# Strassen's seven products for an FFN up projection, and the FFN split into an up phase and a down phase

## The chip, the cores and the metric

One core of a Trainium2 chip runs one inference step of a decoder layer. The metric is the device time of one execution in microseconds, the median of several runs. Matrix products run on TensorE (PE in the profile, its weight loads are PEld), elementwise work on VectorE (DVE), ScalarE (ACT) and GpSimd (POOL); SyncE (SP) issues most DMAs. Matmuls write to PSUM, which the kernel uses in tiles of one or two banks of 512 columns; all else stands in SBUF or in DRAM.

## The reference, cut to what matters

1024 prompt tokens and 8 sample tokens (one each of 8 requests) go through one layer of width 1024. A token mixer (gated delta rule and a convolution branch, merged by gates and projected by `w_out`) is followed by the FFN, in which `T` is 1024 and `D_FF` 2816:

```
x = x + merged @ w_out                         # output projection, residual
h = rmsnorm(x, norm_ffn_w)
u = causal_dwconv(h @ w_up, state, ffn_conv_w) + ffn_conv_b      # width 3 along the tokens, 2*2816 channels
x = x + (silu(u[:, :2816]) * u[:, 2816:]) @ w_down
y = rmsnorm(x, norm_final_w)
```

The last rows of `h @ w_up` are returned as the new convolution state as well. All values are float32.

## The kernel before, in words

Activations lie with channels on the partitions and the 1032 tokens (1024 prompt, 8 sample) along the columns, in three tiles `t` of 344 (`TH`). Every large product is done in three terms: each operand is split into a high part, rounded to the type float32r, and a low part, and `gemm` (L172, its matmul at L182) adds high x high, low weight x high and high weight x low for each 128 rows k of the contraction. A weight tile (8 k of 128x128, 512 KB) comes in two DMAs and is split by `split_w` (L135): ScalarE makes the high part (L140), VectorE the low part (L141).

Matmuls are issued in the order in which the program writes them. A background job (a generator such as `norm2`) writes its own matmuls between those of a gemm: `tick()` (L152) is called after every fourth matmul, and a job that yields n goes on 2n ticks later. The other engines and the DMA queues are ordered by a planner, which takes what it reckons ready, in written order where several are; an engine then works its list strictly in that order, and an instruction that waits holds up those behind it. Tiles of a closed pool give their memory to the pools opened after it; a new tile waits until the readers of the old tiles under it are through.

The output projection (L1171 to L1181) runs t by t over 8 output tiles m; x1 (the residual stream) stays in SBUF. After each t `norm2(t)` (L1155) is spawned: column sums by TensorE, a reciprocal root on VectorE, a broadcast by TensorE, then the scaling and the split into h2hi and h2lo.

The FFN goes through its 22 channel tiles f. `up_pair(f)` (L1245) multiplies two weight tiles, the gate's and the value's, with all three token tiles, each gemm into one PSUM bank out of six (`mmtile2`); ScalarE copies each bank into rg or rv and makes the third tap on the way (L1209, L1210). `up_taps` (L1217) adds the other two taps on VectorE, the sample tokens get theirs from the state, ScalarE applies silu (L1257), VectorE multiplies and splits into yh and yl. After every second tile, `down_mt` (L1301, matmul L1308) adds the previous two tiles' share of the down projection onto x1, for 8 m and 3 t; the last four tiles come at the end, t by t, and `final` (L1328) normalizes each t and stores it.

Of the kernel before, what the change touches and what calls it, by code (L numbers as in the profile page):

```python
# [16 lines left out]
P = 128  # L17
# [17 lines left out]
EPS = 1e-6  # L35
MAGIC = 1597463007.0
# [15 lines left out]
    wod=(KT, P, KT, P), woc=(KT, P, CI, P), wout=(KT, P, KT, P), wup=(2 * NF, P, KT, P), wdn=(NF, P, KT, P),  # L52
# [10 lines left out]
def body(tc, I, O):  # L63
# [20 lines left out]
    with top:  # L84
# [3 lines left out]
        wp = top.enter_context(tc.tile_pool(name="wp", bufs=2, side="left", **R))  # L88
        ap = top.enter_context(tc.tile_pool(name="act", bufs=1, side="left", **R))
        mmp = top.enter_context(tc.tile_pool(name="mmp", bufs=2, space=PSUM, **R))  # L90
# [147 lines left out]
        d_vn = dram.tile([NH, NB, P], F32, name="d_vn")  # L238

# [819 lines left out]
        mhi = [ap.tile([P, KT, TH], F32R, tag=f"ahi{t}", name=f"mhi{t}") for t in range(NTH)]  # L1059
        mlo = [ap.tile([P, KT, TH], F32R, tag=f"alo{t}", name=f"mlo{t}") for t in range(NTH)]  # L1060
# [21 lines left out]
        for m in range(KT):  # L1082
# [13 lines left out]
            if m == KT - 2:  # L1096
                finish(cj)
                cst.close()
                load_c0()
        sas = (("raw", 2), ("zs", 1), ("raw", 2), ("xs", 1))  # L1100
        for m in range(KT):
            w = next_w()
            for t, (t0, n, npr) in enumerate(th):
                sg = sgp.tile([P, TH], F32, tag="sg", name="sgb")
                nc.sync.dma_start(sg, d_gb[m, :, t0:t0 + TH])
                g, bufs = sas[(NTH * m + t) % 4]
                sa = hp.tile([P, TH], F32, tag=g, name="sa", bufs=bufs)
                nc.sync.dma_start(sa, d_ga[m, :, t0:t0 + TH])
                ps = mmtile()
                gemm(ps, w, ((lambda k: chi[t][k]), (lambda k: clo[t][k])), CI)  # L1110
                stt(sg, sg, 1.0, ps, ALU.add, ALU.mult)
                add(sg, sg, sa)
                nc.scalar.activation(mhi[t][:, m, :], sg, AF.Copy, scale=0.5)
                stt(mlo[t][:, m, :], sg, 0.5, mhi[t][:, m, :].bitcast(F32), ALU.mult, ALU.subtract)
# [5 lines left out]
        fst = ExitStack()  # L1120
        rp_ = fst.enter_context(tc.tile_pool(name="res", bufs=1, side="right", **R))
        x1 = [rp_.tile([P, KT, TH], F32, name=f"x1_{t}") for t in range(NTH)]
        nsp = fst.enter_context(tc.tile_pool(name="nsp", bufs=1, side="right", **R))
        mm2 = fst.enter_context(tc.tile_pool(name="mm2", bufs=4, space=PSUM, **R))
        psn2 = fst.enter_context(tc.tile_pool(name="psn2", bufs=1, space=PSUM, **R))
        alt = dict(i=0)

        def psc_():
            return psn2.tile([P, 3], F32, tag="nrm_c", name="nrm_c")

        def psb_():
            return psn2.tile([P, TH], F32, tag="nrm_b", name="nrm_b")


        def mmtile2():
            alt["i"] += 1
            return (mmp if alt["i"] % 3 == 0 else mm2).tile([P, TH], F32, tag="mm", name="mm")

        nacc = [None] * NTH

        def sq_acc(t, src, m, key):
            if m == 0:
                nacc[t] = nsp.tile([P, TH], F32, tag="nacc", name="nacc", bufs=2)
                nc.scalar.activation(nacc[t], src, AF.Square)
            else:
                sq = nsp.tile([P, TH], F32, tag="nsq", name="nsq", bufs=2)
# [3 lines left out]
        ost = ExitStack()  # L1150
        op_ = ost.enter_context(tc.tile_pool(name="op", bufs=2, side="right", **R))
        wo = [None] * KT
        h2hi, h2lo = [None] * NTH, [None] * NTH

        def norm2(t):  # L1155
            yield 3
            rb = yield from col_rsqrt_g(nsp, psc_, psb_, nacc[t], TH, 1.0 / D)
            h2hi[t] = ap.tile([P, KT, TH], F32R, tag=f"ahi{t}", name=f"h2hi{t}")
            h2lo[t] = ap.tile([P, KT, TH], F32R, tag=f"alo{t}", name=f"h2lo{t}")
            for k in range(KT):  # L1160
                hh = nsp.tile([P, TH], F32, tag="hh", name="hh", bufs=2)
                stt(hh, x1[t][:, k, :], nrm[:, 1, k:k + 1], rb, ALU.mult, ALU.mult)
                split(h2hi[t][:, k, :], h2lo[t][:, k, :], hh)

        n2j = None

        def load_wo(m):
            wo[m] = load_w(I["wout"][m], wp) if m < 2 else load_w(I["wout"][m], op_, f"oh{m}", f"ol{m}", 1)

        load_wo(0)  # L1170
        for t, (t0, n, npr) in enumerate(th):  # L1171
            for m in range(KT):
                if t == 0 and m + 1 < KT:
                    load_wo(m + 1)
                xs = op_.tile([P, TH], F32, tag="xs", name="xs")
                nc.sync.dma_start(xs, I["xT"][m, :, t0:t0 + n])
                ps = mmtile2()
                gemm(ps, wo[m], ((lambda k: mhi[t][:, k, :]), (lambda k: mlo[t][:, k, :])), KT)
                add(x1[t][:, m, :], ps, xs)
                sq_acc(t, x1[t][:, m, :], m, "n2")  # L1180
            n2j = spawn(norm2(t))  # L1181
        ost.close()

# [9 lines left out]
        G = 2  # L1193
        ups = [I["wup"][i] for i in range(2 * NF)]
        yh, yl, wd = {}, {}, {}
        upw = {}

        def get_up(i):
            if i < 2 * NF and i not in upw:
                upw[i] = load_w(ups[i], wp)  # L1200

        def h2rhs(t):
            return (lambda k: h2hi[t][:, k, :]), (lambda k: h2lo[t][:, k, :])

        def up_mm(i, raw, acc):
            nc.gpsimd.memset(raw[:, 0:FW - 1], 0.0)

            def ev(t, ps, t0, n, npr):
                nc.scalar.copy(raw[:, FW - 1 + t0:FW - 1 + t0 + npr], ps[:, 0:npr])  # L1209
                nc.scalar.activation(acc[:, t0:t0 + npr], ps[:, 0:npr], AF.Identity, bias=cfb[:, i:i + 1],  # L1210
                                     scale=cfw[:, i, 2:3])
                if t == 2:
                    nc.scalar.copy(stf[:, i, :, FW - 1], ps[:, npr:n])  # L1213

            return ev

        def up_taps(i, raw, acc, lo=0, hi=T):  # L1217
            for j in (1, 0):
                stt(acc[:, lo:hi], raw[:, lo + j:hi + j], cfw[:, i, j:j + 1], acc[:, lo:hi], ALU.mult, ALU.add)
            if hi < T:  # L1220
                return
            nc.gpsimd.tensor_copy(fpo[:, i, :], raw[:, T:T + FW - 1])
            pr = fp_.tile([P, NB, FW], F32, tag="fpr", name="fpr", bufs=2)
            mul(pr, stf[:, i], cfw[:, i, :].unsqueeze(1).to_broadcast([P, NB, FW]))
            nc.vector.tensor_reduce(out=acc[:, T:NT], in_=pr, op=ALU.add, axis=mybir.AxisListType.X)
# [226 lines left out]
```

## Time and profile before

| | us |
|---|---|
| median of 3 runs (lowest, highest) | 1866.91 (1866.83, 1866.99) |
| span of the profiled execution | 1863.8 |
| TensorE busy in it | 1836.3 |
| VectorE, ScalarE, GpSimd busy | 1245.1, 824.1, 101.4 |

The profiled execution is one of its own; its span is the time from its first to its last instruction, and the device time of a run has a few microseconds around it. A busy matmul record covers the time to its modelled end, so neighbouring records overlap; the time that one adds to a stream is the distance from its start to the next start.

### The profile page before, as it was taken

Reading aid. Unit: us, or ns where it says so; the run is one execution under the profiler, and the core shown is the slowest. Engines: PE = TensorE matmul, PEld = TensorE weight load, DVE = VectorE, ACT = ScalarE, POOL = GpSimd, SP = SyncE. Lnnn points to the kernel's source line nnn. Section 1 sums busy time; section 2 is a strip of 40 time slices with the busy share of each in tenths; the row PEclk is TensorE's granted clock in tenths of the full one; section 3 lists DMA queues with packets and bytes.
Section 4 is the critical chain, followed back from the end, with each engine's and each line's share of the span. In section 5 each row is a group of like instructions: output and inputs, shape, how many; then the busy total and the mean of one; then the engine's idle time right before and its main releaser. Section 6 shows DMA issues by size and latency. Waiting matters only on the chain.

```text
span 1863.8 us, 33240 instructions
## 1 busy us (share of the span) xinstructions
PE 1836.3 (99%) x12607; PEld 1816.9 (97%) x12607; DVE 1245.1 (67%) x3222; ACT 824.1 (44%) x2090; POOL 101.4 (5%) x245
## 2 busy tenths in 40 slices
PE   7999999999999999999999999999999999999997
PEld 7899999999999999999999999999999999999997
DVE  7998798689868986745447556445545545555567
ACT  5565456555655565544223235242243243234241
POOL 4300020001000100000000000000000000000000
PEclk9999999999999999999999999999999999999999
DMA  4233213222322243335556212011011011012012
GB/s 163 64 124 103 88 69 118 89 75 86 123 91 75 88 128 96 114 121 176 165 180 204 93 62 74 18 68 52 18 68 58 23 57 69 22 47 68 34 48 92
DMA packets 114112, 163.66 MB, mean 88 GB/s; under 512 B 31968, under 2 KB 68768, under 8 KB 113952
## 3 DMA queue, kind: packets, MB, share of 16 engines
q1 hardware_dynamic: 106896, 153.07, 25.3%
q10 hardware_dynamic: 7056, 8.47, 1.3%
q8 instruction: 99, 1.62, 0.4%
q14 instruction: 61, 0.50, 0.1%
HBM read 128.20 MB, written 33.29 MB: 87 GB/s over the span
## 4 chain that ended last, share of the span: by engine, by line
PE 93%; DVE 4%; ACT 1%; DMA 1%; issue 0%; SPq 0%; DVEq 0%; ACTq 0%
PE mm L182 71%; PE mm L1308 13%; PE tr L659 1%; PE tr L746 1%; PE psS L824 1%; DVE cacc L78 1%; PE po L831 1%; PE tr L724 1%; PE pv L815 1%; PE po L821 1%; PE pk L810 1%; DVE xt L78 1%; PE tr L787 0%; PE tr L797 0%; PE tr L901 0%
## 5 line engine op out<-in xcount | busy, mean ns | idle before, releaser
L182 PE MATMUL mm<-hhi,whi 128*128 128x344 f32 x1360 | 449.8, 331 | 11.4 <-ACT whi L81 6.9
L182 PE MATMUL mm<-hhi,wlo 128*128 128x344 f32 x1360 | 449.7, 331 | 2.5 <-DVE wlo L75 2.4
L182 PE MATMUL mm<-hlo,whi 128*128 128x344 f32 x1360 | 440.3, 329 | 0.0
L182 PE MATMUL mm<-h2hi,whi 128*128 128x344 f32 x1056 | 337.2, 319 | 0.0
L182 PE MATMUL mm<-h2hi,wlo 128*128 128x344 f32 x1056 | 336.6, 319 | 0.0
L182 PE MATMUL mm<-h2lo,whi 128*128 128x344 f32 x1056 | 336.3, 319 | 0.0
L140 ACT CAST whi<-wraw 128x512 fp32r<-128x512 f32 x276 | 164.6, 626 | 308.3 <-PE mm L1308 188.3
L182 PEld LDWEIGHTS mm<-hhi,whi 128*128 128x128 f32 x1360 | 258.9, 190 | 15.3 <-ACT whi L81 7.4
L182 PEld LDWEIGHTS mm<-hhi,wlo 128*128 128x128 f32 x1360 | 259.0, 190 | 4.8 <-DVE wlo L75 3.7
L182 PEld LDWEIGHTS mm<-hlo,whi 128*128 128x128 f32 x1360 | 257.2, 190 | 0.5
L141 DVE TENSOR_TENSOR wlo<-wraw,whi 128x512 fp32r<-128x512 f32 x272 | 184.7, 688 | 96.7 <-ACT whi L140 94.8
L72 DVE TENSOR_TENSOR x<-x,mm 128x344 f32<-128x344 f32 x240 | 120.4, 511 | 137.8 <-PE mm L1308 137.8
L182 PEld LDWEIGHTS mm<-h2lo,whi 128*128 128x128 f32 x1056 | 198.2, 188 | 0.0
L182 PEld LDWEIGHTS mm<-h2hi,whi 128*128 128x128 f32 x1056 | 198.2, 188 | 0.0
L182 PEld LDWEIGHTS mm<-h2hi,wlo 128*128 128x128 f32 x1056 | 198.2, 188 | 0.0
L78 DVE SCALAR_TENSOR_TENSOR cacc<-u,ccw,cacc 128x512 f32<-128x512 f32 x240 | 172.9, 743 | 0.6 <-ACT cacc L563 0.5
L1308 PE MATMUL mm<-yh,whi 128*128 128x344 f32 x480 | 153.3, 319 | 0.0
L1308 PE MATMUL mm<-yl,whi 128*128 128x344 f32 x480 | 153.3, 319 | 0.0
L1308 PE MATMUL mm<-yh,wlo 128*128 128x344 f32 x480 | 153.0, 319 | 0.0
L182 PE MATMUL mm<-og,whi 128*128 128x344 f32 x512 | 123.2, 321 | 0.0
L78 DVE SCALAR_TENSOR_TENSOR ag<-rg,cfw,ag 128x1024 f32<-128x1024 f32 (+2 forms) x48 | 57.3, 1195 | 49.4 <-ACT stf L1213 48.3
L1308 PEld LDWEIGHTS mm<-yh,whi 128*128 128x128 f32 x480 | 90.3, 188 | 0.0
(325 smaller groups left out, 3046.5 us busy)
## 6 DMA issues: line engine op xcount, KB each, us to landing
wraw<-in_wup SPq DMA_DIRECT2D x88, 256.0 KB, 2.6
wraw<-in_wdn SPq DMA_DIRECT2D x44, 256.0 KB, 2.7
gr<-d_gc SPq DMA_DIRECT2D x16, 512.0 KB, 3.7
xt<-in_xT SPq DMA_DIRECT2D x12, 344.0 KB, 6.4
d_ga<-sg ACTq DMA_DIRECT2D x24, 172.0 KB, 2.1
d_gb<-sg ACTq DMA_DIRECT2D x24, 172.0 KB, 1.9
sga<-d_ga SPq DMA_DIRECT2D x24, 172.0 KB, 2.3
d_ga<-sga SPq DMA_DIRECT2D x24, 172.0 KB, 3.8
```

What stands on the lines that cost most here:

```text
L72: nc.vector.tensor_tensor(out=out, in0=a, in1=b, op=ALU.add)
L78: nc.vector.scalar_tensor_tensor(out=out, in0=a, scalar=s, in1=b, op0=op0, op1=op1)
L140: nc.scalar.copy(hi[:, k:k + 4], raw)
L141: weng["e"].tensor_tensor(out=lo[:, k:k + 4], in0=raw, in1=hi[:, k:k + 4].bitcast(F32), op=ALU.subtract)
L182: nc.tensor.matmul(ps, lhs[:, k, :], r(k), start=k == 0 and i == 0, stop=k == kt - 1 and i == 2)
L659: nc.tensor.matmul(gv[:, i, :], kT[:, cs[c]], kT[:, cs[c]], start=True, stop=True)
L724: nc.tensor.matmul(gv[:, i, :], kT[:, cs[c]], qT[:, cs[c]], start=True, stop=True)
L746: nc.tensor.transpose(gv[:, i, :], src[:, cs[half * 4 + i]], ident)
L810: nc.tensor.matmul(pk, kT[:, cs[c]], S, start=True, stop=True)
L815: nc.tensor.matmul(pv, tt[:, c, :], vs[:, c, :], start=True, stop=True)
L821: nc.tensor.matmul(po, qT[:, cs[c]], S, start=True, stop=False)
L1308: nc.tensor.matmul(ps, w, y[f][:, t0:t0 + TH], start=n == 0, stop=n == last)
```

## The change: what it does

Let the up weights of a channel tile be cut in four: the gate's and the value's 128 columns, each in an upper and a lower half of the contraction (4 k each): a21 and a22 of the gate, a11 and a12 of the value. The tokens are cut into two halves b of 516 and each of these into two quarters of 258 (`Q`), so that the normalized input has four blocks for each b. Strassen's scheme in its form by Winograd gets the four output blocks (gate and value, by two quarters) from seven block products in place of eight: sums s1 to s4 of weight pieces, differences t1 to t4 of input blocks (b11, t2, b21, t3, t1, t4, n22 in the order of use), and sums of the products. `prod` issues one product for the halves b in its list, 12 matmuls of 258 columns each; products go to three PSUM tiles x, y, z of two banks (one bank for each b), some of them added onto what stands there after that has been read: the order is x, y, x, y, z, y, z, and after the products p1s, u2, c11, u3, c22, c21 and c12 are formed in turn (`EV`). c11 and c12 are value blocks (tile rv), c21 and c22 gate blocks (tile rg).

The output projection works with the same quarters, m by m for each half b: 258 columns instead of 344, its weights loaded once for each b, and it also writes the residual stream to DRAM (`d_x1`). `norm2(b)` then scales X[b] in place and `combos(b)` forms the seven operands, each with a high and a low part; those of b=1 are formed while the first pass runs. That pass is begun with b=0 alone. The activated y of each channel tile goes to DRAM (`d_y`); the sample tokens' taps are formed once at the end for all tiles. After the last tile the up phase's memory is given up, and the down phase runs t by t with the whole contraction in two units of 11 channel tiles (33 matmuls of 344 columns each), h=1 of a tile two steps behind h=0. y is read back from DRAM and split there, the down weights (in a new layout, by output tile) are read and split again for each t, and the residual comes from `d_x1`.

The mixer before it changes only in where mhi and mlo (the output projection's input) stand and how they are cut. The core of the diff:

```diff
+Q = NT // 4
+HB2 = 2 * Q
+KH = KT // 2
+FH = NF // 2
...
+        def norm2(b):
             yield 3
+            p1, p2 = norm_ps()
+            rb = yield from col_rsqrt_g(nsp, p1, p2, nacc[b], HB2, 1.0 / D)
             for k in range(KT):
+                stt(X[b][:, k, :], X[b][:, k, :], nrm[:, 1, k:k + 1], rb, ALU.mult, ALU.mult)
+            if tpool[b] is not None:
+                yield 2
+                yield from combos(b)
...
+        def get_wq(f, j):
...
+            nm = ORD[j][0]
+            if nm[0] == "s":
+                if nm == "s2":
+                    get_sum(f, "s1")
+                src = get_sum(f, nm)
+            else:
+                src = raws[f, nm]
+            h = up_.tile([P, KH, P], F32R, tag="uhi", name="uhi", bufs=7)
+            l = up_.tile([P, KH, P], F32R, tag="ulo", name="ulo", bufs=7)
+            split(h, l, src)
+            wq[f, j] = (h, l)
+
+        def prod(f, j, z, bs, start, stop):
+            wh, wl = wq[f, j]
+            nm = ORD[j][1]
+            for b in bs:
+                n = 0
+                for k in range(KH):
+                    for w, r in ((wh, That), (wl, That), (wh, Tlot)):
+                        nc.tensor.matmul(z[:, b, 0:Q], w[:, k, :], r[b][nm][:, k, :], start=start and n == 0,
+                                         stop=n == 3 * KH - 1, skip_group_check=True)
+                        n += 1
+                        if n % 4 == 0:
+                            tick()
...
+        EV = (e_p1, e_u2, e_c11, e_u3, e_c22, e_c21, e_c12)
+        DST = ("x", "y", "x", "y", "z", "y", "z")
...
+        u = begin(0)
+        for j in range(6):
+            stage(u, j, (0,), j not in (2, 4, 5))
+        finish(n2j[1])
+        nst.close()
...
+        fp_ = fst.enter_context(tc.tile_pool(name="ffn", bufs=1, side="right", **R))
...
+        outs(u)
+        s0 = slice(0, 1)
+        e_c11(u, s0)
+        e_c22(u, s0)
+        e_c21(u, s0)
+        stage(u, 6, (0,))
+        for j in range(7):
+            stage(u, j, (1,))
+            get_wq(1, j)
+        get_raw(2)
+        activate(u)
+        for f in range(1, NF):
+            u = begin(f)
+            outs(u)
+            for j in range(7):
+                stage(u, j, (0, 1))
+                get_wq(f + 1, j)
+            get_raw(f + 2)
+            activate(u)
...
+        for i in range(len(seq)):
...
+            t, m, h = seq[i]
...
+            for f in range(FH):
+                for w, y in ((wh, yh), (wh, yl), (wl, yh)):
+                    nc.tensor.matmul(ps, w[:, f, :], y[:, f, :], start=h == 0 and n == 0,
+                                     stop=h == 1 and n == 3 * FH - 1)
```

## Rows read from the trace of the kernel before

**Rows 1.** The page: busy time of the engines, and TensorE's clock in 40 slices.
```profile
PE 1836.3 (99%) x12607; PEld 1816.9 (97%) x12607; DVE 1245.1 (67%) x3222; ACT 824.1 (44%) x2090; POOL 101.4 (5%) x245
...
PEclk9999999999999999999999999999999999999999
```

**Rows 2.** The page: the chain of waits, share of the span by engine.
```profile
PE 93%; DVE 4%; ACT 1%; DMA 1%; issue 0%; SPq 0%; DVEq 0%; ACTq 0%
```

**Rows 3.** Windows (us, then engines busy, clock, DMA share, GB/s): output projection, FFN, within.
```profile
1010.00:1101.00 91.00, 91.00 (x590) 91.00 (x590) 52.10 (x125) 29.87 (x58) 0.00 (x0) 1.00 0.33 104
1101.00:1850.20 749.20, 749.20 (x4789) 748.66 (x4788) 410.57 (x736) 261.30 (x514) 12.89 (x87) 1.00 0.14 49
1200.00:1800.00 600.00, 600.00 (x3831) 600.00 (x3830) 319.58 (x539) 204.41 (x398) 9.97 (x69) 1.00 0.14 48
```

**Rows 4.** Groups by line: output projection, one of three kinds; busy us, mean ns.
```profile
L182 PE MATMUL mm<-mhi,whi 128*128 128x344 f32 x192 | 61.5, 320 | 0.0
```

**Rows 5.** Timeline of TensorE at the kernel's start, at half clock: start, length.
```profile
17.16 0.49 PE L182 MATMUL mm<-hhi,wlo 128*128 128x344 f32 x1
17.45 0.49 PE L182 MATMUL mm<-hhi,whi 128*128 128x344 f32 x1
```

**Rows 6.** Timeline of weight loads after two matmuls of 2 columns.
```profile
767.06 0.19 PEld L182 LDWEIGHTS mm<-hhi,whi 128*128 128x128 f32 x1
767.17 0.19 PEld L182 LDWEIGHTS mm<-hhi,wlo 128*128 128x128 f32 x1
```

**Rows 7.** Timeline of weight loads: between them runs an ordinary-float matmul of 258 columns.
```profile
765.26 0.19 PEld L182 LDWEIGHTS mm<-hhi,wlo 128*128 128x128 f32 x1
765.48 0.19 PEld L182 LDWEIGHTS mm<-hlo,whi 128*128 128x128 f32 x1
```

**Rows 8.** DMA issues: KB each, median us to landing.
```profile
wraw<-in_wup SPq DMA_DIRECT2D x88, 256.0 KB, 2.6
```

**Rows 9.** Groups of ScalarE instructions by form: busy us, mean ns.
```profile
L140 ACT CAST whi<-wraw 128x512 fp32r<-128x512 f32 x276 | 164.6, 626 | 308.3 <-PE mm L1308 188.3 <-PE mm L182 59.0 <-DMA wraw<-in_wdn 25.8
L1209 ACT COPY rv<-mm 128x344 f32<-128x344 f32 x35 | 15.6, 445 | 39.4 <-PE mm L182 39.3
L1257 ACT ACTIVATE ag<-ag 128x1032 f32<-128x1032 f32 x21 | 22.4, 1068 | 12.9 <-DVE ag L1226 12.9
L563 ACT ACTIVATE cacc<-u,ccv,ccw 128x1024 f32<-128x1024 f32 x4 | 5.0, 1242 | 0.1
```

**Rows 10.** Groups of VectorE instructions by form: busy us, mean ns.
```profile
L72 DVE TENSOR_TENSOR x<-x,mm 128x344 f32<-128x344 f32 x240 | 120.4, 511 | 137.8 <-PE mm L1308 137.8
L141 DVE TENSOR_TENSOR wlo<-wraw,whi 128x512 fp32r<-128x512 f32 x272 | 184.7, 688 | 96.7 <-ACT whi L140 94.8
L78 DVE SCALAR_TENSOR_TENSOR hh<-x,nrm,nrm_b 128x344 f32<-128x344 f32 x16 | 8.6, 566 | 1.1 <-PE nrm_b L219 0.9
L78 DVE SCALAR_TENSOR_TENSOR av<-rv,cfw,av 128x1024 f32<-128x1024 f32 x42 | 53.8, 1280 | 40.2 <-ACT stf L1213 40.2
L69 DVE TENSOR_TENSOR av<-av,ag 128x1032 f32<-128x1032 f32 x21 | 25.8, 1230 | 0.4
```

**Rows 11.** Timeline of VectorE: two low halves in a row.
```profile
1301.92 1.29 DVE L141 TENSOR_TENSOR wlo<-wraw,whi 128x512 fp32r<-128x512 f32 x2 [1.70 <-ACT whi L140]
```

**Rows 12.** Timeline of TensorE after an idle, and the window behind it (clock, DMA, GB/s last).
```profile
57.95 0.42 PE L182 MATMUL mm<-hhi,whi 128*128 128x344 f32 x1 [1.46 <-ACT bas L1003]
...
59.30:62.60 3.30, 3.30 (x15) 3.24 (x14) 3.11 (x9) 0.52 (x2) 2.03 (x2) 0.50 0.45 149
```

**Rows 13.** Timeline of ScalarE in an up pass: waits in brackets.
```profile
1311.98 1.05 ACT L81 CAST yh<-av 128x1032 fp32r<-128x1032 f32 x1 [2.18 <-DVE av L69]
1312.94 0.63 ACT L1210 ACTIVATE ag<-mm,cfb,cfw 128x344 f32<-128x344 f32 x1
```

**Rows 14.** The page: DMA busy tenths and rate in 40 slices.
```profile
DMA  4233213222322243335556212011011011012012
GB/s 163 64 124 103 88 69 118 89 75 86 123 91 75 88 128 96 114 121 176 165 180 204 93 62 74 18 68 52 18 68 58 23 57 69 22 47 68 34 48 92
```

More of the change, by code (lines that the diff above doesn't have):

```diff
@@ L1056, in body @@
             tick()
-        mhi = [ap.tile([P, KT, TH], F32R, tag=f"ahi{t}", name=f"mhi{t}") for t in range(NTH)]
-        mlo = [ap.tile([P, KT, TH], F32R, tag=f"alo{t}", name=f"mlo{t}") for t in range(NTH)]
+        mhi, mlo = [None] * 2, [None] * 2
         c0st = ExitStack()
@@ L1098, in body @@
                 cst.close()
+                ast.close()
+                mp = wst.enter_context(tc.tile_pool(name="mrg", bufs=1, side="left", **R))
+                for b in (1, 0):
+                    mhi[b] = mp.tile([P, KT, HB2], F32R, name=f"mhi{b}")
+                    mlo[b] = mp.tile([P, KT, HB2], F32R, name=f"mlo{b}")
                 load_c0()
@@ L1117, in body @@
         hs.close()
[L1120 to L1129, printed above, removed]
@@ L1170, in body @@
         load_wo(0)
-        for t, (t0, n, npr) in enumerate(th):
+        load_wo(1)
+        n2j = [None, None]
+        for b in range(2):
+            X[b] = xpool[b].tile([P, KT, HB2], F32, name=f"x{b}")
             for m in range(KT):
[L1173 to L1181, printed above, removed]
@@ L1182, in body @@
-        ost.close()
+                load_wo(KT * b + m + 2)
+                xs = nsp.tile([P, HB2], F32, tag="xs", name="xs", bufs=2)
+                nc.sync.dma_start(xs, I["xT"][m, :, b * HB2:(b + 1) * HB2])
+                ps = pw.tile([P, 2, 512], F32, tag="mm", name="mm")
+                for j in range(2):
+                    sl = slice(j * Q, j * Q + Q)
+                    gemm(ps[:, j, 0:Q], wo[KT * b + m],
+                         ((lambda k: mhi[b][:, k, sl]), (lambda k: mlo[b][:, k, sl])), KT)
@@ new lines, in body, with get_raw @@
+        up_ = ust.enter_context(tc.tile_pool(name="upw", bufs=1, side="left", **R))
+        n2j[1] = spawn(norm2(1))
+        raws, sums = {}, {}
+        wq = {}
+        def get_raw(f):
+            if f >= NF:
+                return
+            for nm, i, h in (("a11", 1, 0), ("a21", 0, 0), ("a22", 0, 1), ("a12", 1, 1)):
+                r = up_.tile([P, KH, P], F32, tag="raw", name="raw", bufs=5)
+                nc.sync.dma_start(r, I["wup"][2 * f + i][:, KH * h:KH * h + KH, :])
+                raws[f, nm] = r
@@ new lines, in body, with small, ptile @@
+        get_raw(0)
+        for j in range(7):
+            get_wq(0, j)
+        get_raw(1)
+        pt_ = tmpp
+        def small(f):
+            return [pt_.tile([P, 2, Q], F32, tag=g, name=g, bufs=1) for g in ("p1s", "u2", "u3")]
+        alt = dict(i=0, pool=None)
+        def ptile():
+            alt["i"] += 1
+            if alt["pool"] is not None and alt["i"] % 4 == 0:
+                return alt["pool"].tile([P, 2, 512], F32, tag="mm", name="mm")
+            return pw.tile([P, 2, 512], F32, tag="mm", name="mm")
@@ new lines, in body, with views, begin, outs @@
+        fp_ = None
+        def views(raw):
+            return raw[:, FW - 1:FW - 1 + NT].rearrange("p (b h c) -> p b h c", b=2, h=2)
+        class Tile_:
+            pass
+        def begin(f):
+            u = Tile_()
+            u.f, u.x, u.y, u.z = f, ptile(), ptile(), ptile()
+            u.p1s, u.u2, u.u3 = small(f)
+            return u
+        def outs(u):
+            u.rg = fp_.tile([P, FW - 1 + NT], F32, tag="rg", name="rg")
+            u.rv = fp_.tile([P, FW - 1 + NT], F32, tag="rv", name="rv")
+            u.ag = fp_.tile([P, T], F32, tag="ag", name="ag")
+            u.av = fp_.tile([P, T], F32, tag="av", name="av", bufs=2)
+            nc.gpsimd.memset(u.rg[:, 0:FW - 1], 0.0)
+            nc.gpsimd.memset(u.rv[:, 0:FW - 1], 0.0)
+            u.vg, u.vv = views(u.rg), views(u.rv)
@@ L1346, in body @@
         finish(fj)
-        fst.close()
+        dst_.close()
 def _const():
```

386 lines of the change are left out of this document (228 added, 158 removed).

## The prediction

> **What bounds the kernel now.** I read the page's busy shares and clock first [rows 1]: TensorE is busy 99% of the span and its granted clock stands at 0.9 or more in every slice. The chain of waits says the same, 93% of it is TensorE [rows 2]. The windows then give the part that is changed [rows 3]: from 1101.00 to 1850.20 us (the FFN) and in the output projection before it TensorE is busy for the whole stretch, while VectorE is busy 410.6 of 749.2 us and ScalarE 261.3. So nothing but TensorE's stream counts there today; each matmul removed is worth its start-to-start time, and each new wait of TensorE costs its full length. The price of one: the FFN's 749.20 us hold 4789 matmuls, 156.4 ns each, and the 600.00 us within it 3831, 156.6; a few are norm matmuls [rows 3]. I use 0.1563 us. The recorded 320 ns of one [rows 4] is longer because matmuls overlap.
>
> **The stream of matmuls.** Before, an up pass (one of 22) has 2 weights x 3 token tiles x 8 k x 3 split terms = 144 matmuls of 344 columns, 3168 in all: 495.2 us. The down projection has 8 x 3 x 22 x 3 = 1584: 247.6 us. The output projection has 576, 192 of each kind [rows 4]: 90.0 us. After, a pass has 7 products x 2 token halves x 4 k x 3 terms = 168 matmuls of 258 columns, 3696 in all; down stays at 1584 of 344; the output projection becomes 2 x 8 x 2 x 24 = 768 of 258. Columns fall by an eighth in the up projection and by nothing elsewhere; the count rises. So all hangs on what a 258-column matmul of this type costs, and no row of before has one. Bounds: scaled by columns from 344 it is 156.3 x 258/344 = 117.2 ns. If instead the 12.9 ns above 344 columns at 2.4 GHz (143.3 ns) is a fixed part, it is 107.5 + 12.9 = 120.4 ns. At 1.2 GHz the same form runs 287 ns apart, exactly its columns with nothing on top [rows 5], which speaks for neither: whatever costs the 12.9 ns shows at the high clock alone. Below, the weight loads set a floor: after two matmuls of 2 columns the next two loads start 0.11 us apart [rows 6]. An ordinary-float matmul of 258 columns has 0.22 us from load to load [rows 7]: twice 258 columns at 2.4 GHz is 215 ns, so it looks like two streamings of 110 ns or less, almost without a fixed part. Above, if the load of 128 weight columns and the moving columns share one supply, 472 columns in 156.3 ns make 386 columns 127.8 ns. I take the middle of the two extrapolations of the same form, 118.8 ns; ends 111 and 128. The up projection is then 439.1 us (-56.1) and the output projection 91.2 us (+1.2): -54.9 us for the stream.
>
> The Trainium skill ("TensorE: Matmul & The Clock Gate", Back-to-back issue gap) puts neighbouring matmuls at the high clock N / 2.4 + 2.5 ns apart. It would make 344 columns 145.8 ns, and the trace shows 156.3; for 258 columns it gives 110.0 ns, about the floor above. By that rule the stream would gain 39 us more than my sum; the rival "floor" below has its chance.
>
> **The start of the up phase.** TensorE takes its work in written order, so this is where the change adds waits. Call the last output-projection matmul W.
> The first weight piece (a11 of pass 0) goes into memory that still holds the low halves of the second token half, read by the very last matmul. So its DMA starts at W: 2.6 us to landing [rows 8], 0.63 us cast [rows 9], some signals: TensorE starts again at about W + 3.7. Before, it went from one gemm to the next without idle.
> The program then runs products 1 to 6 of pass 0 for the first token half alone, 72 matmuls, 8.6 us, with the second half's norm inside: its column sums after 28 matmuls, its broadcast after 60. With a little waiting for the sums that form the Strassen weights (each 0.69 us on VectorE [rows 10]) the broadcast stands at about W + 14. VectorE now multiplies 8 tiles of 516 columns (0.57 us for 344 columns [rows 10], slope 1.05 ns per column, less what neighbours overlap: 0.66, so 5.3 us) and forms the seven token operands: 8 differences and 14 low halves, 22 operations of 516 columns at 0.62 = 13.6 us. Two low halves of 512 columns in a row took 1.29 us, 0.645 each [rows 11], hence 0.62 to 0.65. That ends at W + 33.
> Product 7 adds to the accumulator z that held product 5, and so waits until VectorE has read it (block c22). That read writes the tile rg, and rg stands in the memory of the second half's x, which is read until the last of the 22 operations. So TensorE stands from about W + 15 to W + 34. Of these 34 us 8.6 are matmuls of the sum and 2.2 norm matmuls that exist before too: 23 us lost. After an idle of 1.46 us and some small matmuls the clock stood at 0.50 for 3.3 us [rows 12], which costs half of that: 2 us. After the wait VectorE has some 17 us of work (the rest of pass 0, weights of pass 1, activation) beside 96 matmuls, 11.4 us: I put 3 us (0 to 6) for it. Sum +28. The norm of the second half is covered by nothing here; before, the last norm of the three ran beside two thirds of the first up tiles.
>
> **The steady passes.** One pass is 168 x 0.1188 = 20.0 us of TensorE. VectorE has 4 sums and 7 low halves of weights (11 x 0.645 = 7.1), 5 block evictions (516 columns, 0.65 each, 3.3), 4 taps (1.28 us, some 1.21 in a row [rows 10]: 4.8) and the gate product 1.15: 16.3 us, 82%. ScalarE: 7 casts at 0.6, 2 copies at 0.59, 2 scaled copies at 1.24, silu 1.07, about 9 us [rows 9]. So neither is a bound. But x, y and z are each read and added to again with one product, 2.85 us, in between; before, six banks stood in rotation and a late eviction cost nothing. The taps of the pass before fall on products 1 and 2; counted in written order, VectorE's read of y after product 2 ends about 1 us before product 4 needs it. The order is a planner's, and an engine waits at the head of its queue: in a pass of before ScalarE stood 2.18 us for the cast yh, with an eviction ready behind it [rows 13]. I take 0.3 us a pass, +6 us (0 to 45).
>
> **From up to down.** Weights for down can be loaded early; y comes back from DRAM. The first piece, 704 KB, can start when product 6 of the last pass is done. At some 340 GB/s (the page's busiest slice moved 204 GB/s at 0.6 [rows 14]) and a 2 us delay it lands 1 us after the last up matmul. Then cast (1.4 us) and low half (1.6 us, both scaled from the 1032-column rows, [rows 9, 10]) stand beside 6.6 us of the last activation and 3 us for the sample tokens on VectorE. Down's first unit (33 matmuls, 5.2 us) needs 4.4 us of low halves of y and 1.6 of weights; I put its end 8 us late (5 to 17, the long end if the read must wait until the sample columns are written). Pass 21's own y is needed 15.6 us later, after three units: hidden. In steady down a unit loads 704 KB in 5.2 us, 140 GB/s, with y and residual about 220; 0.6 of what the queues can do, so it fits. The second halves of y have one buffer, loaded during three units: 1 us for each of two turns, +2. The first output-projection gemm now takes a PSUM bank that the last merge gemm has just used: +1. The removed work on VectorE (per-pass sample taps, x adds per group) was hidden and gains nothing. The tail after the last matmul keeps its form: 13.6 us from 1850.2 to the end.
>
> **Sum.** -54.9 + 28 + 6 + 8 + 2 + 1 = -9.9 us. The profiled span goes from 1863.8 to 1853.9; the median of the runs is 3.1 us above that span, so 1866.9 - 9.9 = 1857 us.
>
> **Rivals.**
> *Floor*: narrow matmuls cost 111 ns. For it: the loads of [rows 6] and the 110 ns of [rows 7]; against it: the 156.3 ns, where the same load has room enough and there is still 12.9 ns on top. 4464 x 7.8 ns = 35 us less: 1822 us.
> *Short start*: the norm of the second half doesn't hold product 7 (rg placed clear of it, or the 22 operations largely ahead): 20 us less, 1837. Against it: the pool of rg opens where that of x was closed.
> *Evictions become the bound* (the slower side): in each pass products 3 to 6 wait for a read of y or x queued behind taps and splits. Place: the first third of a pass; price up to what the activation takes beyond two products. From 0.8 us a pass (0.5 over my 0.3) the gain is gone; at 2 us a pass it is +36: 1893. For it: the head-of-queue wait of [rows 13] and 82% of VectorE; against it: 1 us of slack by written order.
> *Shared supply*: 128 ns a matmul: 4464 x 9.2 = +41, 1898. For it: the 12.9 ns, which no row explains; against it: the ordinary-float matmul of 258 columns loads as many weights and shows no such part [rows 7].
>
> **Chances.** Forecast 0.45 (its own range 1838 to 1876: 3 ns either way on 4464 matmuls is 13 us, the waits some 10), floor 0.13, short start 0.10, evictions 0.21, shared supply 0.11. A measurement of this kernel tells 0.2%, 3.7 us, from no change. Of the forecast's 0.45, 0.31 is faster, 0.06 the same, 0.08 slower; with the rivals: faster 0.54, same 0.08, slower 0.38. Eight in ten: 1820 to 1895.
>
> **What would show it.** Matmuls of 258 columns 117 to 120 ns apart in the middle of the up phase, and a pass of 20 us; one long idle of TensorE some 15 us after the output projection that ends with VectorE's c22 on rg, and one shorter before a11; in steady passes waits of TensorE on p1s, u2, u3 or c22 summing to under 10 us; an idle of 5 to 10 us before the first down matmul that ends with y. It is wrong if the gap is 111 or 128, if the long idle is under 10 us, or if the waits inside passes reach 20 us in all.

## The result, and the profile of the changed kernel

The changed kernel takes 1877.3 us (median of 4 runs, 1875.4 to 1878.9) against 1866.9: ratio 1.0055, 95% interval 1.0041 to 1.0070, slower by 10.4 us. The profiled span is 1873.6 us against 1863.8. The forecast was 1857 us. Its sign was wrong; the measured time lies inside the span of eight in ten (1820 to 1895) and 1 us beyond the forecast's own range (1838 to 1876).

From the page: TensorE's busy time, its clock in 40 slices, and the chain of waits by engine. They answer to [rows 1, 2]:
```profile
PE 1793.1 (96%) x13331; PEld 1770.8 (95%) x13331; DVE 1360.8 (73%) x3146; ACT 869.9 (46%) x1999; POOL 121.8 (7%) x245
...
PEclk9999999999999999999999998999999999899998
...
PE 88%; DVE 5%; DMA 2%; ACT 2%; issue 2%; SPq 0%; POOLq 0%; DVEq 0%; POOL 0%; ACTq 0%
```
TensorE has 43 us less to do, and yet the end is 10 us later: its share fell from 99 to 96%, and the clock has three slices at 0.8 where it had none (the last of them at the very end). The windows show where [rows 3]; the columns are those of before (output projection, start of the up phase, the rest of it, turn to down, down):
```profile
1009.00:1104.30 95.30, 94.74 (x788) 94.52 (x788) 58.50 (x108) 32.93 (x60) 0.00 (x0) 1.00 0.51 160
1104.30:1145.00 40.70, 16.02 (x101) 14.52 (x100) 32.64 (x66) 13.67 (x24) 0.20 (x2) 0.73 0.27 87
1145.00:1579.70 434.70, 434.70 (x3619) 434.70 (x3617) 343.35 (x443) 191.94 (x298) 29.33 (x85) 1.00 0.22 75
1579.70:1603.00 23.30, 0.43 (x3) 0.22 (x3) 18.14 (x19) 11.24 (x11) 1.17 (x1) 0.59 0.83 279
1603.00:1860.00 257.00, 254.53 (x1608) 253.28 (x1608) 125.20 (x146) 87.95 (x82) 0.00 (x0) 0.99 0.57 186
```
For 434.7 us of the up phase TensorE never stops: 3619 matmuls, 120.1 ns each. The loss is in two places, the 40.7 us at its start and the 23.3 us at its end, both at a lower mean clock. What TensorE waited for, by the line that released it (us in total, times, longest):
```profile
PE mm L1520 <- ACT wdh L85: 22.9, 1, 22.9
PE mm L1301 <- ACT rv L1354: 17.6, 1, 17.6
PE mm L1301 <- ACT uhi L85: 5.8, 2, 3.5
```
L1301 are the up products, L1520 the down projection. The first row is the wait for the down weights, the second the wait of product 7 of the first pass, the third the waits for the first two weights of the up phase.

The terms of the sum, against the forecast. W is the start of the last output-projection matmul (1104.15 us); the FFN before was 749.2 us, of which 742.8 are its matmuls by the forecast's count, so 6.4 were something else.

| term | forecast | measured | how |
|---|---|---|---|
| output projection | +2.2 | +3.3 | ends at 1104.3, before 1101.0; 1.5 of it is there at its first matmul already (1009.6, before 1008.1) |
| matmuls of the up projection | -56.1 | -51.3 | 3696 x 0.1201 - 495.2 |
| start and passes, beyond the matmuls | +34 | +31.6 | 475.5 from W to the last up matmul, less 443.9 |
| turn to down | +8 | +23.2 | 1579.63 to 1602.79 |
| within down, beyond before | +2 | +2.9 | 256.9 - 247.6 - 6.4 |
| sum | -9.9 | +9.7 | spans: +9.8 |

### The profile page after: what moved, and what is told of

Read it like the earlier page. It is cut to its first block, busy times and chain, and to the rows that moved or that the text cites. A ratio compares the mean times of both kernels' runs of the same rounds, so it can differ in the third digit from the quotient of the medians.

```text
span 1873.6 us, 34767 instructions
## 1 busy us (share of the span) xinstructions
PE 1793.1 (96%) x13331; PEld 1770.8 (95%) x13331; DVE 1360.8 (73%) x3146; ACT 869.9 (46%) x1999; POOL 121.8 (7%) x245
## 4 chain that ended last, share of the span: by engine, by line
PE 88%; DVE 5%; DMA 2%; ACT 2%; issue 2%; SPq 0%; POOLq 0%; DVEq 0%; POOL 0%; ACTq 0%
PE mm L187 44%; PE mm L1301 23%; PE mm L1520 11%; DMA draw<-in_wdn 1%; PE psS L831 1%; PE tr L666 1%; PE tr L731 1%; PE tr L753 1%; PE po L838 1%; PE pv L822 1%; DVE wdl L79 1%; PE po L828 1%; PE pk L817 1%; DVE xt L82 1%; PE tr L794 0%
## 5 line engine op out<-in xcount | busy, mean ns | idle before, releaser
L1301 PE MATMUL mm<-h_t,uhi 128*128 128x258 f32 x704 | 199.5, 283 | 2.3 <-ACT uhi L85 2.3
L1301 PE MATMUL mm<-h_t,ulo 128*128 128x258 f32 x704 | 199.7, 284 | 0.1
L1301 PE MATMUL mm<-l_t,uhi 128*128 128x258 f32 x704 | 199.6, 284 | 0.0
L1520 PE MATMUL mm<-yh,wdh 128*128 128x344 f32 x528 | 170.0, 322 | 22.9 <-ACT wdh L85 22.9
L1520 PE MATMUL mm<-yh,wdl 128*128 128x344 f32 x528 | 169.6, 321 | 0.7 <-DVE wdl L79 0.7
L1520 PE MATMUL mm<-yl,wdh 128*128 128x344 f32 x528 | 169.7, 321 | 0.0
L1301 PEld LDWEIGHTS mm<-h_t,uhi 128*128 128x128 f32 x704 | 133.6, 190 | 2.6 <-ACT uhi L85 2.6
L1301 PEld LDWEIGHTS mm<-h_t,ulo 128*128 128x128 f32 x704 | 133.4, 190 | 0.4 <-DVE ulo L79 0.4
L1301 PEld LDWEIGHTS mm<-l_t,uhi 128*128 128x128 f32 x704 | 133.6, 190 | 0.0
L1520 PEld LDWEIGHTS mm<-yh,wdh 128*128 128x128 f32 x528 | 100.0, 189 | 23.1 <-ACT wdh L85 23.1
```

The costliest lines, as they stand in the source:

```text
L1301: nc.tensor.matmul(z[:, b, 0:Q], w[:, k, :], r[b][nm][:, k, :], start=start and n == 0, stop=n == 3 * KH - 1, skip_group_check=True)
L1520: nc.tensor.matmul(ps, w[:, f, :], y[:, f, :], start=h == 0 and n == 0, stop=h == 1 and n == 3 * FH - 1)
```

## The experiments

Times are set beside the kernel before (1866.7 to 1866.9 in each set); the changed kernel stands at 1877.3. W lies between 1103.3 and 1106.6 us in the profiles, so places are counted from each run's own W.

**Theory.** The 23 us at the turn are the order of one DMA queue; the 17.9 us at the start are the memory that rg shares with x. Rivals: the loads wait for data or memory, and the start is bound by VectorE's work.

### The turn

The issues of SP's queue at the turn in the changed kernel (start, length, operation):
```profile
1576.95 0.37 SPq L1459 DMA_DIRECT2D yl<-d_y  x1
1582.37 0.34 SPq L1428 DMA_DIRECT2D out_fp<-fpo  x1
1582.80 0.39 SPq L1429 DMA_DIRECT2D out_fs<-stf  x1
1583.24 2.00 SPq L1459 DMA_DIRECT2D yl<-d_y  x3
1588.84 0.33 SPq L1391 DMA_DIRECT2D d_y<-av  x1
1589.22 0.43 SPq L1459 DMA_DIRECT2D yl<-d_y  x1
1593.45 0.36 SPq L1439 DMA_DIRECT2D d_y<-yd  x1
1593.90 1.69 SPq L1459 DMA_DIRECT2D yl<-d_y  x1
1595.65 0.95 SPq L1468 DMA_DIRECT2D draw<-in_wdn  x2
```
The down weights (draw) are the last to leave, 16.0 us behind the last up matmul, although no engine has to compute them. Ahead of them stand writes that wait: the state output (out_fp) 5.0 us for GpSimd's copy, the last pass's y (d_y<-av) 3.5 us for VectorE's gate product, and the sample columns (d_y<-yd) 3.7 us for VectorE. The chain of waits goes exactly there:
```profile
1593.45 0.36 SPq L1439
...
1595.65 5.70 DMA draw<-in_wdn
1601.35 0.02 issue
1601.37 1.37 ACT wdh L85
```

**weights_first**
```
-        load_y(0, 0)
         loaded = 0
         AHEAD = 2
+        while loaded < AHEAD + 1:
+            load_d(*seq[loaded])
+            loaded += 1
+        load_y(0, 0)
```


> The down weights of the first three units are asked for ahead of y instead of behind it; nothing else changes. Theory (queue order): the 23 us idle between the phases is the weights' DMAs standing in SyncE's queue behind the writes of the last y and of the sample columns (10 us behind when they go out at 1595.65). Then TensorE starts on y alone, about 1588 instead of 1603, the half clock afterwards is shorter, and the kernel takes 1861 to 1866 us. Rival (the round trip of y and VectorE's last activation set the idle): y is then as late as the weights were, the idle stays over 18 us, 1873 to 1878 us.

Measured 1871.9 us (8 runs; ratio to before 1.0030, 1.0020 to 1.0041). That is 5.4 us less than the changed kernel, but neither the theory's range (1861 to 1866) nor the rival's (1873 to 1878). The wait fell from 22.9 to 10.3 us, and four rows of 0.6 to 1.0 us appear behind it. The wait, then SP's queue:
```profile
PE mm L1523 <- ACT wdh L85: 10.3, 1, 10.3
```
```profile
1584.70 0.34 SPq L1428 DMA_DIRECT2D out_fp<-fpo  x1
1585.13 0.39 SPq L1429 DMA_DIRECT2D out_fs<-stf  x1
1585.61 1.21 SPq L1468 DMA_DIRECT2D draw<-in_wdn  x2
1591.17 0.33 SPq L1391 DMA_DIRECT2D d_y<-av  x1
1591.55 0.43 SPq L1459 DMA_DIRECT2D yl<-d_y  x1
```
Half the idle went (10.6 us from the last up matmul to the first of down, instead of 23.2), and half of that came back within down (263.1 us instead of 256.9): the weights still stand behind out_fp, and now the rest of y stands behind a write.

**turn_queue**: as weights_first, and the four writes leave by GpSimd's queue (the other two, out_fs and the sample columns of y, are edited alike).
```
-            nc.sync.dma_start(d_y[f, :, 0:T], u.av)
+            (nc.gpsimd if f == NF - 1 else nc.sync).dma_start(d_y[f, :, 0:T], u.av)
...
-        nc.sync.dma_start(O["fp"], fpo)
+        nc.gpsimd.dma_start(O["fp"], fpo)
...
```


> Edit: as weights_first (down weights loaded ahead of y), and the four writes that close the up phase (the two state outputs, the last pass's y rows, the state columns of y) go out on GpSimd's DMA queue instead of SP's. Theory (writes that wait for late results hold the loads behind them in SP's queue): in weights_first the first down weights left at 1585.6 us, 3.6 us after the last up matmul, and the second and third parts of y at 1591.5 us and later, behind such writes. Now both leave by about 1580 us: idle of TensorE between the phases 4 to 7 us instead of 10.6, and the 5.3 us of small waits after it gone; 1861 to 1866 us. Rival (the loads wait for memory or for VectorE's own work of the last pass, not for the queue): idle stays at 9 to 11 us, 1869 to 1872 us.

Measured 1865.7 us (10 runs; 0.9995, 0.9986 to 1.0005), so the same as before and 11.6 us under the changed kernel. SP's queue holds only loads, and the first down weights leave 1.8 us ahead of the last up matmul (1582.82). SP's queue, then the waits at the turn:
```profile
1580.14 0.37 SPq L1459 DMA_DIRECT2D yl<-d_y  x1
1581.02 3.63 SPq L1468 DMA_DIRECT2D draw<-in_wdn  x2
1584.70 0.98 SPq L1459 DMA_DIRECT2D yl<-d_y  x2
```
```profile
PE mm L1523 <- ACT wdh L85: 6.1, 1, 6.1
PE mm L1523 <- DVE yl L79: 2.2, 2, 1.1
PE mm L1523 <- DVE wdl L79: 2.0, 1, 2.0
```
The queue theory holds: the time is in its range, and so is the idle, 6.4 us (4 to 7 said). The small waits behind it, which were to go, are still 4 us. What is left, 10.3 us, is about the forecast's 8: the weights' cast stands behind the last silu and a cast of y on ScalarE, the low halves beside the last activation on VectorE.

### The start

**rg_apart**: the first pass's rg in memory of its own.
```
+        rg0 = up_.tile([P, FW - 1 + NT], F32, tag="rg0", name="rg0", bufs=1)
-            u.rg = fp_.tile([P, FW - 1 + NT], F32, tag="rg", name="rg")
+            u.rg = rg0 if u.f == 0 else fp_.tile([P, FW - 1 + NT], F32, tag="rg", name="rg")
```


> The tile rg of the first pass gets memory of its own instead of that of the second half's x. Theory (memory wait): product 7 of the first half then runs at once, and the second half's products follow the operands as VectorE forms them, the last at about 1143; pass 0 ends near 1145 instead of 1157, and the kernel takes 1864 to 1868 us. Rival (VectorE's 30 operations for the second half bound that stretch wherever rg stands, as the half clock and the backlog behind them do): less than 4 us gained, 1873 us or more.

Measured 1876.4 us (1.0050, 1.0034 to 1.0067): no gain that can be told, the rival's range. **both_apart** does the same to rv.

> Edit: the first pass's two tiles of finished rows, rg and rv, get memory of their own instead of the memory of the second half's x, which the second half's normalisation still reads until about 1143 us. Theory (this shared memory is all that holds TensorE from 1128 to 1143 us): the 14.2 us wait for the ScalarE copy to rv goes. The second half's products are then held by their own operands alone, which VectorE finishes between 1132 and 1145 us, so the first pass ends near 1149 to 1153 us instead of 1166; 12 to 17 us less, 1860 to 1865 us. Rival (VectorE's backlog holds TensorE in any case, since the evictions that free the second half's banks stand behind the operands in VectorE's order): the wait is only split over other rows, 0 to 4 us less, 1873 to 1877 us.

Measured 1879.2 us (1.0067, 1.0052 to 1.0082): no gain either. The longest wait of each at the start, rg_apart first, both_apart second:
```profile
PE mm L1301 <- ACT rv L1356: 14.2, 1, 14.2
```
```profile
PE mm L1301 <- DVE rg L79: 11.2, 1, 11.2
```
In rg_apart product 7 goes through, and the next matmul waits until W + 39.9 (W + 39.3 in the changed kernel) for block c11, whose target rv lies in x too. In both_apart that one goes through, and the next product waits for VectorE's c21 of the first half, which stands behind all operands in VectorE's order. (That a product of the second half waits for a read of the first half, since both are slices of one PSUM tile, is our reading of these two rows.) A guard that is lifted hands the wait to the next one.

The guards are not the whole of it, though. From the first scaling of x to the third pass it takes 52.6 us in the changed kernel, 49.7 in rg_apart and 51.3 in both_apart, so the lifted guards did gain 1 to 3 us there. But the scaling itself began at W + 22.6 in both, instead of W + 20.0, and took the gain back. TensorE ran slower meanwhile: its mean clock in the first 20 us behind W was 0.83 in the changed kernel, 0.66 in rg_apart and 0.74 in both_apart. Why it differed isn't shown.

**raw_early**: the sums s3 and s4 are allocated ahead of the weight pieces, so that these don't lie on the last low halves.
```
+        for nm in ("s3", "s4"):
+            up_.tile([P, KH, P], F32, tag=nm, name=nm, bufs=1)
         get_raw(0)
```


> Two weight sums take the memory over the low halves of the second token half, so that the first weight pieces stand where the first half's stood, which is free 45 us earlier; nothing else changes. Theory: the weights of pass 0 are loaded and split before the output projection ends, the 3.8 us idle before the up phase and the two shorter ones in products 1 and 2 (4 us) go, the norm's broadcast comes 6 to 9 us earlier and with it the end of the long wait: 1867 to 1871 us. Rival (VectorE and ScalarE are held by the last residual and squares, or the DMAs keep their place in the queue): under 3 us, 1874 us or more.

Measured 1878.8 us (1.0068, 1.0053 to 1.0083): nothing gained. a11 leaves 4.3 us ahead of W, the others behind the last write of x1, which SP's queue holds until x is made:
```profile
1100.64 0.38 SPq L1266 DMA_DIRECT2D raw<-in_wup  x1
1106.00 0.33 SPq L1245 DMA_DIRECT2D d_x<-x  x1
1106.38 1.99 SPq L1266 DMA_DIRECT2D raw<-in_wup  x4
```
The first up product starts at W + 2.3 instead of W + 3.8, and the long wait of product 7 stayed (17.6 us by the waits, as in the changed kernel). **all_three** joins weights_first, rg_apart and raw_early.

> The three edits together: weights before y, rg of the first pass apart, first weight pieces early. If the three idles are separate, the gains add up: 12 + 10 + 8 us, 1845 to 1852 us, faster than the kernel before. If they overlap (the second and third both shorten the same stretch that VectorE's operand work bounds), about 20 us: 1855 to 1859 us.

Measured 1871.3 us (1.0023, 1.0011 to 1.0035), outside both ranges: no more than weights_first gave alone (1871.9).

**start_and_turn** joins both_apart, turn_queue and raw_early; the second half's x1 writes leave by GpSimd's queue, the first down loads have priority.

> Edit: both of the others, the second half's writes of x1 on GpSimd's queue with the two sums allocated first so that the first up weights can leave early, and the first loads of the down phase at high priority. If the two theories hold and are independent, the gains add: 12 to 17 us at the first pass, 11 to 16 us at the turn, 1 to 3 us for the earlier first weights: 1843 to 1853 us. If only the queue theory holds: 1860 to 1866 us. If VectorE's backlog decides in both places: 1870 to 1875 us.

Measured 1863.0 us (0.9979, 0.9969 to 0.9988), the range for the queue theory alone. The idle at the turn is that of turn_queue, 6.4 us; all weights of the first pass left 8 to 10 us ahead of W, and at the start the wait of both_apart stays (11.1 us). So memory alone is not what holds the start.

**inline_first**: rg and rv apart, the first half's evictions right behind their products, the second half's products between the operands.
```
-        for j in range(6):
-            stage(u, j, (0,), j not in (2, 4, 5))
+        for j in range(7):
+            stage(u, j, (0,))
+        for j in range(7):
+            while ORD[j][1] not in That[1]:
+                tick()
+            stage(u, j, (1,))
         finish(n2j[1])
...
```


> Edit: rg and rv of the first pass in memory of their own as in both_apart, and now all evictions of the first half stand in the order of the work right behind their products, ahead of the second half's operands; the second half's products follow each operand as it is made, and the splits of the second pass's weights come behind them. Theory (in both_apart VectorE's order alone kept the 11.2 us wait: the evictions stood behind the last operand, while a wait on a bank of x or y in the second half covers the first half's rows of the same tile): the wait of 17.6 us goes, the second half's products end about 3 us after the last operand, which is about 41 us behind the last output-projection matmul, so the first pass ends 44 to 47 us behind it instead of 66; 17 to 22 us less than the changed kernel, 1855 to 1860 us. Rival (VectorE has so much to do there that its backlog comes out at the second pass's weights instead): a new wait at the second pass, 0 to 8 us less, 1869 to 1877 us.

Measured 1875.1 us (1.0038, 1.0024 to 1.0052), the rival's 0 to 8 us. No wait is longer than 4 us now, the first pass ends 4.6 us sooner, and the second stops 3.4 us for VectorE's read u of y, which stands behind the activation.:
```profile
PE mm L1301 <- ACT uhi L85: 6.3, 2, 3.7
PE mm L1301 <- DVE u L79: 3.4, 1, 3.4
```
Here too the scaling began late, at W + 24.0 (clock 0.66 in the first 20 us), and the stretch behind it fell to 49.3 us.

**inline_and_turn** is this with the turn and the early first weights of start_and_turn.

> Edit: inline_first together with the turn of start_and_turn (down weights first, closing writes on GpSimd's queue, first loads of the down phase at high priority) and its earlier first weights. Theory (the two places are independent, and what start_and_turn still lost at the first pass was VectorE's order): 1863.0 us less 14 to 20: 1843 to 1849 us, faster than the kernel before by 1 per cent. Rival (VectorE's backlog comes out elsewhere): 1855 to 1863 us.

Measured 1862.4 us (0.9969, 0.9956 to 0.9982): the rival's range again. Beside inline_first the scaling begins 6.5 us earlier, at W + 17.5 (clock 0.91 in the first 20 us), and the second pass ends 6.4 us earlier.

New theory: from W to the end of the second pass VectorE's work is of one size, and what counts is above all when its main part, from the scaling on, begins. In the changed kernel the norm's scaling of x begins only at W + 20, since the two groups of matmuls that it needs stand behind products that wait for weights. **norm_ahead**, on the changed kernel alone:
```
         n2j[1] = spawn(norm2(1))
+        for _ in range(12):
+            tick()
```


> Edit, the changed kernel with this alone: the second half's sum of squares and its rsqrt stand ahead of the first up product in TensorE's order, and the matmuls that spread the result stand right behind the first product instead of behind the sixth. Theory (the start of the up phase is VectorE's chain of normalisation and operands, which began 20 us behind the last output-projection matmul only because its two small groups of matmuls stood behind products that waited for weights): the scaling of x begins about 12 us behind that matmul instead of 20, TensorE's wait of 17.9 us falls to 8 to 11 us, and the second pass ends 63 to 66 us behind it instead of 72.6; 1867 to 1871 us. Rival (VectorE is short of time in the first two passes whatever the order, as the second pass's waits in inline_first suggest): the wait falls too, but a new one of the same length comes by the end of the second pass: 1874 to 1878 us.

Measured 1872.2 us (8 runs; 1.0025, 1.0015 to 1.0035): 5.1 us less from this edit alone, between the two ranges and 1 us above the theory's. The scaling in VectorE's timeline, in the changed kernel (first row of it) and here, then TensorE's longest waits here:
```profile
1124.20 2.08 DVE L82 SCALAR_TENSOR_TENSOR x<-x,nrm,nrm_b 128x516 f32<-128x516 f32 x3 [1.56 <-PE nrm_b L224]
```
```profile
1117.83 5.38 DVE L82 SCALAR_TENSOR_TENSOR x<-x,nrm,nrm_b 128x516 f32<-128x516 f32 x8
```
```profile
PE mm L1303 <- DVE rg L76: 8.1, 1, 8.1
PE mm L1303 <- DVE u L79: 5.4, 1, 5.4
```
It begins at W + 13.2 instead of 20.0; product 7 waits 8.1 us instead of 17.6, with rg still in the memory of x, and the second pass ends 5.8 us sooner.

**norm_and_all** is inline_and_turn with this.

> Edit: inline_and_turn with the norm of norm_ahead. Theory (the late chain): the second pass ends 58 to 62 us behind the last output-projection matmul instead of 66.7, 5 to 8 us less than inline_and_turn: 1854 to 1858 us. Rival (VectorE short of time whatever the order): 1860 to 1863 us.

Measured 1858.9 us (5 runs, 1852.9 to 1859.9; 0.9951, 0.9938 to 0.9965): less than both kernels, by 8 and 18 us, and 1 us above the theory's range. The profile is that of the fastest of the five runs. The window from W to the start of the third pass, in the changed kernel and here:
```profile
1104.15:1176.70 72.55, 47.87 (x358) 46.30 (x357) 56.79 (x102) 28.05 (x48) 2.73 (x7) 0.84 0.26 82
```
```profile
1104.46:1165.43 60.97, 47.75 (x359) 45.73 (x358) 55.82 (x102) 26.89 (x48) 2.59 (x6) 0.92 0.23 76
```
VectorE has the same 56 us in it, 78% of the stretch there and 92% here; TensorE's 336 up matmuls take 40.4. The same window is 72.2 us long in rg_apart, 73.7 in both_apart, 73.2 in inline_first, 66.8 in norm_ahead and 66.7 in inline_and_turn, with 56.4 to 57.1 us of VectorE in each. From the scaling on VectorE is busy 43.7 of 52.6 us in the changed kernel and 46.3 of 47.9 here: only here does it work nearly without a gap. That its work bounds the stretch is thus measured for this last kernel; for the others, with gaps of 6 to 9 us, it is our reading.

### The matmul of 258 columns

**width_probe**: rows of matmuls with changing weights behind the end.
```
+            for k in range(c):
+                nc.tensor.matmul(pz[:, 0:w], zr[:, 512 + 128 * (k % 16):640 + 128 * (k % 16)], zr[:, 0:w],
+                                 start=k == 0, stop=k == c - 1)
```


> Edit: the changed kernel with rows of matmuls added behind its end, each with another weight tile, after a warm-up of 160 matmuls of 512 and 160 of 344 columns; then 96 each of 128, 172, 258, 300, 344, 430 and 512 columns, and 258 again; read by the trace as the distance from start to start. Theory of a fixed part (12.9 ns on top of the columns at 2.4 GHz, from 156.3 ns at 344 and 120.3 at 258): 300 columns 137.9, 430 columns 192.1, 512 columns 226.2 ns. Rival, a proportional law (1.090 times the columns at 2.4 GHz, from 344 columns): 258 columns 117.2, 430 columns 195.4, 512 columns 232.6 ns. A floor by the weight loads, which followed each other no closer than 0.11 us: then 128 and 172 columns both take about 107 to 112 ns, against 66 and 85 ns by the fixed part.

One run. Windows of 128, 172, 258, 300, 344, 430 and 512 columns (fields as above; the length by the count gives the gap, but for two matmuls at the edges):
```profile
1936.00:1945.00 9.00, 9.00 (x83) 9.00 (x82) 0.00 (x0) 0.00 (x0) 0.00 (x0) 1.00 0.01 2
1946.00:1956.00 10.00, 10.00 (x92) 10.00 (x91) 0.16 (x1) 0.00 (x0) 0.00 (x0) 1.00 0.00 0
1957.00:1968.00 11.00, 11.00 (x94) 11.00 (x93) 0.01 (x1) 0.00 (x0) 0.00 (x0) 1.00 0.00 0
1969.00:1981.00 12.00, 12.00 (x89) 12.00 (x88) 0.00 (x0) 0.00 (x0) 0.00 (x0) 1.00 0.00 1
1982.00:1996.00 14.00, 14.00 (x91) 14.00 (x90) 0.00 (x0) 0.00 (x0) 0.00 (x0) 1.00 0.01 1
1997.00:2015.00 18.00, 18.00 (x93) 17.38 (x92) 0.00 (x0) 0.00 (x0) 0.00 (x0) 1.00 0.00 1
2016.00:2036.00 20.00, 20.00 (x90) 16.53 (x89) 0.00 (x0) 0.00 (x0) 0.00 (x0) 1.00 0.00 0
```
From start to start the means of the rows are 111.1, 111.9, 120.1 (of two rows), 137.8, 157.7, 196.7 and 227.2 ns. Above the columns at 2.4 GHz that is 12.6 at 258, 12.8 at 300, 14.4 at 344 and 13.9 at 512 columns: nearer to a fixed part than to the proportional law, which would have 232.6 ns at 512. It is no constant: the 344 columns of the warm-up took 153.3 ns (10.0 above), and the 430 columns (17.5) fit neither law; why stays open. 128 and 172 columns cost the same: the floor.

## Why the prediction was wrong

*The stream of matmuls.* The middle of two extrapolations was taken, 118.8 ns; the upper one, the fixed part (120.4), was right for 258 columns. 3696 matmuls x 1.3 ns make 4.8 us, and the output projection 1 us. The ordinary-float pair of [rows 7], which spoke for almost no fixed part, was no guide to the other type. The floor of [rows 6] exists, but lies below 258 columns; the rivals "floor" and "shared supply" are out.
The Trainium skill ("TensorE: Matmul & The Clock Gate", Back-to-back issue gap) gives N / 2.4 + 2.5 for a matmul by itself and says that a stream with weight loads is spaced otherwise, a condition that the prediction left out. The formula would have 110.0 ns at 258 and 215.8 at 512 columns; this case's streams with weight loads show 120 and 227, so here the measurement decides. Its rule for the low clock, N / 1.2, agrees: 215 ns, and 0.21 to 0.22 us from start to start behind the wait of product 7.

*The start of the up phase.* Near in size, in part by luck: start and passes together lost 31.6 us against 28 + 6, but all of it up to the third pass (72.7 us from W to there, of which the 336 up matmuls take 40.4; the norm's own matmuls are in the rest), while the 6 of the passes did not come. Right in what the trace shows: the first product at W + 3.8 (3.7 said), then product 7 stood from W + 21.4 to W + 39.3, 17.9 us, until c11 and c22 went behind the last operand. But the cause given was only the first of three guards. Lifting rg's memory (rg_apart), then rv's too (both_apart), then changing the order (inline_first) left the end of the second pass where it was, 72.2 to 73.7 us behind W, partly since the scaling began later in these runs. An edit that only begins the norm earlier moved that end by 5.8 us. So the rival "short start" was priced wrongly: clear memory for rg alone gave nothing that can be told, not 20 us. The norm's broadcast came at W + 18.5 rather than W + 14: the first six products waited longer for their weights than said, and some of their matmuls ran at the lower clock.

*The steady passes.* +6 was set; TensorE shows no wait inside a pass in 434.7 us, with VectorE at 79% of it, and the last 20 passes took 402.8 us, 119.9 ns a matmul. The rival "evictions" is out.

*From up to down.* This is the step that failed, with 15 us (23.2 against 8, and outside its range of 5 to 17): "Weights for down can be loaded early". They were not: the DMAs left SP's queue in the order shown above, and the weights stand in the last of its nine lines, behind writes that wait for GpSimd and VectorE. The prediction weighed when y could come back and what the engines had to do, and never laid the entries of the queue out in order; it named "the long end if the read must wait until the sample columns are written" for y, and it was the weights that waited. With the order mended (turn_queue) the idle is 6.4 us; of the 16.8 us that it lost, 3.6 came back within down (260.6 us instead of 256.9), so that turn and down together stand 3 us above the 8 + 2 forecast. The 8.7 us that turn_queue lies above the forecast are in the main the 6 of the matmuls and these 3: the turn made the kernel slower, and even with it mended the forecast gain of 10 us was not there. None of the three signs that the prediction gave for being wrong came (the gap is 120 ns, the long idle 17.9 us, the passes wait for nothing): the loss stood at a place that none of its rivals named.

*Within down*: +2.9 against +2; the matmuls after the restart ran at half clock for 5 us, and before them TensorE had stood for 23 us.

## What to carry to other kernels

Between two fixed points add up each engine's work before pricing single waits: where another engine's sum (here 56 us) exceeds TensorE's (40), a lifted guard may only move the wait, as it did here three times, and beginning that engine's chain earlier can be worth more (5 us here, by one edit). At a change of phase write out each DMA queue's entries in order and ask of every one what it waits for; a load that nothing delays belongs ahead of a write that waits, or in another queue. A narrower matmul of this type saved its columns and not the part on top of them: a quarter fewer columns saved 36 of 156 ns, which over 3696 matmuls is 11 us short of a quarter.

## What the runs showed of the hardware

- A float32r matmul with a new weight tile cost its columns at 2.4 GHz plus 12.6 to 14.4 ns at 258, 300, 344 and 512 columns in the rows of width_probe (17.5 at 430, 10.0 in the warm-up at 344), and no less than 111 ns (128 and 172 columns alike). At half clock 258 columns are 0.215 us apart (the changed kernel behind the wait of product 7), with nothing on top.
- A long idle cost more than its length: in the changed kernel, behind the 23.2 us in which TensorE did nothing, the first 5.2 us of down ran at the lower of the two clocks (window, clock third from the end):
```profile
1602.80:1608.00 5.20, 4.48 (x14) 4.04 (x15) 3.47 (x3) 2.71 (x2) 0.00 (x0) 0.50 1.02 328
```
- Issuing a write from GpSimd's queue takes that engine 0.5 to 1.4 us in turn_queue, against 0.33 to 0.39 us for the same writes in SP's in the changed kernel. No wait of TensorE at the turn names GpSimd there.
